# Attention of the last two layers as 26 bursts in a written TensorE order, its normalisation on GpSimd, and the value projection later

## The chip, the cores and the metric

The kernel runs on one core of a Trainium2 chip. A core has TensorE (PE, matrix products into the PSUM banks), VectorE (DVE), ScalarE (ACT), GpSimd (POOL) and SyncE (SP, which here issues the loads of the weights). Each engine runs its own queue of instructions in order; semaphores tie them together. The metric is the device time of one execution in microseconds, as a median of runs.

## The reference

Four layers on a sequence of 256 tokens of width 1024, all in fp32. The first two (a mixer of pooling and attention, a gated recurrence, each with a convolutional feed-forward part) are not touched. The change is in the mixer of the last two, `hybrid_layer`:

```python
proj = h @ w_in        # h = rms_norm(x); 6.3 thousand columns, split into the parts below
c_q, c_kv, k_r, d_q, d_k, d_v, s_q, s_k, s_v, gate_logits = jnp.split(proj, offs, axis=-1)
q = (rms_norm(c_q, g_q_lora) @ w_uq)            # MLA: 8 heads of 64 + 32, low rank
kv = (rms_norm(c_kv, g_kv_lora) @ w_ukv)        # keys and values of MLA; then norms and rope
o_mla = mla_attention(q, k, v_mla)              # softmax(q k^T) v, 8 heads
od = diff_attention(dq, dk, dv, ..., lam)       # (softmax_0 - lam softmax_1) v, 4 heads of 128
o_win = window_attention(wq, wk, wv, ..., sink) # band of 128, sinks, 8 query heads on 2 key heads
merged = gates[0] * (o_mla @ w_branch[0]) + gates[1] * (o_diff @ w_branch[1]) \
       + gates[2] * (o_win @ w_branch[2])       # gates = sigmoid(gate_logits)
x = x + merged @ w_out
```

After it come a feed-forward part and a gated addition, which are not touched.

## The kernel before

**Weights.** All weights of the kernel stand in one array in the order in which they are used (`_stream`), cut into chunks of at most 128 x 2048 elements. `_push` loads a chunk (SP's queue), and casts it into a high and a low half in fp32r: ScalarE writes `hi` (L260), VectorE the rest `lo` (L261), each in two pieces. `chunk` hands out the next one and keeps two ahead; `st`, `hi` and `lo` have three buffers each. A product (`mm3`, L277 to L279) is three fp32r matmuls: high by high, high by low, low by high.

**Order.** The program gives no order between independent instructions. A planner, with its own estimate of costs, gives each engine, step by step, the first instruction in program order whose inputs its estimate has as ready; what comes out is the fixed queue of that engine. `InOrder` is a wrapper that pins an instruction behind the one traced before it on its engine. Before, TensorE is pinned nowhere in the mixer but for the matmuls within one `chained`, so the planner strews the gates' products among the attention.

**The mixer, `hybrid`.** In program order: norm, the low-rank projection (`mla_prep`), diff queries and keys (`proj` with `headnorm`), transposes of the low-rank vector (`mla_low_rank`, L954 to L957: ScalarE writes the high half, VectorE the low half), the diff values `dv`, the MLA heads (`mla_heads`), the window keys and values (`window_kv`, keys with `headnorm`), the window queries `wq`, and then the attention: MLA in 4 pairs of heads, differential attention in 2 pairs, the windows in 4 pairs. For each pair: transposes of queries and keys (`qk_T`, L860), scores (`scores` L878, `scores2` through `chained` L870), a softmax (VectorE finds the maximum, L905 or, with a bias, L909; ScalarE the exponentials and their sums, L913; VectorE the reciprocal, L917), a normalisation on ScalarE (L922), transposes of the probabilities (`transpose4`, L849) that ScalarE copies out of PSUM (L851), and the products with the values (`pv2`, L870 and L1080). Biases are made on GpSimd (L895). After that follow the gates (12 products of 8 x 2 x 3 matmuls) and the three branches, in the order of `MERGE`: gate 0, gate 1, branch 0, gate 2, branch 1, branch 2.

`headnorm` (L426 to L431) is: squares on ScalarE, a sum on VectorE, a reciprocal root of eleven tiny instructions (L330, L317, L322 to L324 three times), and a multiplication.

**Buffers.** PSUM has 8 banks: A 3 (weight products), S 2 (scores), T 2 (transposes), O 1 (outputs). Of the SBUF tiles that matter here, `s` (probabilities) has 4 buffers, `qk` 2, `pT` 2, `bias` 2, `o` 4, `hg` 8.

Of the kernel before, what the change touches and what calls it, by code (L numbers as in the profile page):

```python
# [19 lines left out]
P = 128  # L20
S = 256
# [43 lines left out]
def _stream(a):  # L65
# [11 lines left out]
    for i in range(2):  # L77
# [131 lines left out]
class Net:  # L209
    def __init__(self, ctx, tc, ap, out, shapes, vat, rat, upto=99):  # L210
# [6 lines left out]
        self.ph = "s"  # L217
        self.vec_o, self.act_o = InOrder(tc, self.nc.vector), InOrder(tc, self.nc.scalar)
# [56 lines left out]
    def mm3(self, out, ah, al, bh, bl, start, stop):  # L275
        mm = self.nc.tensor.matmul
# [62 lines left out]
    def first_norm(self):  # L339
# [6 lines left out]
        for n in range(2):  # L346
            for t in range(2):
                pt = self.bank("ST"[t])
                for e in range(4):
                    k = 4 * n + e  # L350
                    nc.tensor.transpose(pt[:, e * P:e * P + P], self.x[:, t, k * P:k * P + P], self.ident)
# [14 lines left out]
    def norm(self, gi, banks=None, update=None):  # L366
# [7 lines left out]
        for n in range(2):  # L374
            for t in range(2):
                update(t, n, banks)
            for kp in range(2):
                pt = self.bank("ST"[kp])
                for e in range(2):
                    k = 4 * n + 2 * kp + e  # L380
                    for t in range(2):
                        nc.tensor.transpose(pt[:, e * S + t * P:e * S + t * P + P], self.x[:, t, k * P:k * P + P], self.ident)
# [19 lines left out]
    def norm_rows(self):  # L402
# [4 lines left out]
        for t in range(2):  # L407
            nc.scalar.activation(dg[:, t, :], self.ident, AF.Copy, scale=self.r[:, t:t + 1])
            nc.tensor.matmul(pb[:, t * P:t * P + P], self.ones, dg[:, t, :], start=True, stop=True)
# [58 lines left out]
    def pool_attn(self):  # L468
# [20 lines left out]
        for dst, z, tag, scale in ((qT, qk[0], "S", gqk), (kT, qk[1], "T", None)):  # L489
            for t in range(2):  # L490
                pt = self.bank(tag)
                for c in range(4):
                    nc.tensor.transpose(pt[:, c * P:c * P + P], z[:, t, c * P:c * P + P], self.ident)
# [8 lines left out]
        for c in range(4):  # L502
# [16 lines left out]
            for s in probs:  # L519
                pt = self.bank("T")  # L520
                for j in range(3):
                    nc.tensor.transpose(pt[:, j * P:j * P + P], s[:, j * P:j * P + P], self.ident)
# [21 lines left out]
        for gi in range(4):  # L544
            pb = self.bank("S")
            gc = slice(gi * P, gi * P + P)
            nc.tensor.matmul(pb[:, 0:S], u[:, 0, gc], mt[:, gi, 0:S], start=True, stop=False)
            nc.tensor.matmul(pb[:, P:S], u[:, 1, gc], mt[:, gi, S:384], start=False, stop=True)
# [3 lines left out]
            nc.tensor.matmul(pb2[:, 0:S], pw[:, gi, :], pooled, start=True, stop=True)  # L552
# [133 lines left out]
    def rglru(self, gi):  # L686
# [20 lines left out]
        for jp in range(5):  # L707
# [3 lines left out]
            for e in range(2):  # L711
# [3 lines left out]
                nc.tensor.matmul(pb[:, :S], wa[:, j, :], xc, start=True, stop=True)  # L715
                nc.tensor.matmul(pb[:, S:], wx[:, j, :], xc, start=True, stop=True)
# [126 lines left out]
    def transpose4(self, p):  # L843
# [3 lines left out]
        for kb in range(2):  # L847
            for t in range(2):
                nc.tensor.transpose(pt[:, kb * S + t * P:kb * S + t * P + P], p[:, t * S + kb * P:t * S + kb * P + P], self.ident)  # L849
# [4 lines left out]
    def qk_T(self, q, k, d, gain):  # L854
# [3 lines left out]
        for j, src in enumerate((q, k)):  # L858
            for t in range(2):
                nc.tensor.transpose(pt[:d, j * S + t * P:j * S + t * P + P], src[t], self.ident)  # L860
# [5 lines left out]
    def chained(self, mms):  # L866

        last = None
        for out, lhsT, rhs, start, stop in mms:
            ins = self.nc.tensor.matmul(out, lhsT, rhs, start=start, stop=stop)  # L870
# [4 lines left out]
    def scores(self, qT, kT):  # L875
        sp = self.bank("S")
        for t in range(2):
            self.nc.tensor.matmul(sp[:, t * S:t * S + S], qT[:, t * P:t * P + P], kT, start=True, stop=True)  # L878
# [68 lines left out]
    def mla_low_rank(self, i, c):  # L947
# [3 lines left out]
        for k in range(3):  # L951
            pt = self.bank("ST"[k % 2])
            for t in range(2):
                nc.tensor.transpose(pt[:, t * P:t * P + P], c[:, t, k * P:k * P + P], self.ident)  # L954
# [61 lines left out]
    def mla(self, q4, k4, v):  # L1016
        nc = self.nc
        v_ = nc.vector
        oh, ol = self.t([P, 4, S], "o", F32R), self.t([P, 4, S], "o", F32R)
        for cc in range(4):  # L1020
            ob = self.bank("O")
            probs = []
            for h in (2 * cc, 2 * cc + 1):
                qk = self.qk_T([q4[:, t, h, :] for t in range(2)], [k4[:, t, h, :] for t in range(2)], 96, self.gm)
                probs.append(self.softmax(self.scores(qk[:96, :S], qk[:96, S:]), FULL))
            self.pv2(ob, probs, [v[:, :, h * 64:h * 64 + 64] for h in (2 * cc, 2 * cc + 1)])
            self.split(oh[:, cc, :], ol[:, cc, :], ob[:, :S])
        return oh, ol

    def pv2(self, ob, probs, vs):  # L1030

# [236 lines left out]
```

## Time and profile before

| | |
|---|---|
| median of 3 runs | 1526.07 us (1525.44 to 1526.26) |
| the profiled execution, its own time | 1526.14 us |
| its span, first to last instruction | 1524.0 us |
| TensorE busy | 1505.0 us, 99% of the span |
| VectorE busy | 1136.7 us, 75% |
| ScalarE busy | 940.6 us, 62% |
| GpSimd busy | 53.4 us, 4% |
| granted clock of TensorE | full over the span but for its last microsecond |

Busy times are sums of the instructions' durations; a matmul's end is modelled, and the next one starts before it. The distance between two starts therefore tells more of TensorE's pace than its busy time does. In the rows below PE is TensorE's matmul, PEld its weight load, and what stands after an arrow (`<-ACT s L922`) is the instruction that ended a wait.

### The profile page before, as it was taken

What the parts mean: (1) busy time and instruction counts of PE and PEld (TensorE: products, weight loads), DVE (VectorE), ACT (ScalarE), POOL (GpSimd) and SP (SyncE); (2) the same over time, 40 slices, a digit from 0 to 9 for tenths busy, and PEclk for the clock granted to TensorE, in tenths of its full rate; (3) what the DMA queues carried; (4) which work ended last, traced back from release to release, by engine and by line L of the source; (5) the groups of instructions that cost most, each with busy time, mean ns of one, the idle gap of its engine ahead of it and who ended that gap; (6) DMA issues with size and microseconds to landing.
All of it is one profiled execution on the core that took longest, in us unless ns stands there. A gap on an engine that the chain in (4) does not pass through costs nothing.

```text
span 1524.0 us, 25331 instructions
## 1 busy us (share of the span) xinstructions
PE 1505.0 (99%) x10020; PEld 1354.2 (89%) x10020; DVE 1136.7 (75%) x2197; ACT 940.6 (62%) x1683; POOL 53.4 (4%) x45
## 2 busy tenths in 40 slices
PE   8999999999999999999999999999999999999998
PEld 6789999898999998888898999988888888999986
DVE  6559777789897777876767776668886767866666
ACT  6756555685775556677665655456777674654554
POOL 0200000000000000001110000000000110000000
PEclk9999999999999999999999999999999999999999
DMA  8445555445465554432444555444542335454551
GB/s 300 161 169 189 194 194 173 160 139 193 140 221 173 192 178 173 168 138 86 156 144 172 187 190 193 174 170 173 172 166 96 143 115 194 166 194 172 189 193 55
DMA packets 37878, 257.33 MB, mean 169 GB/s; under 512 B 4384, under 2 KB 4768, under 8 KB 8320
## 3 DMA queue, kind: packets, MB, share of 16 engines
q1 hardware_dynamic: 36576, 252.38, 46.9%
q0 software_dynamic: 896, 3.28, 0.7%
q8 instruction: 78, 1.28, 0.3%
q14 instruction: 40, 0.33, 0.1%
q10 hardware_dynamic: 288, 0.07, 0.0%
HBM read 254.66 MB, written 1.05 MB: 168 GB/s over the span
## 4 chain that ended last, share of the span: by engine, by line
PE 86%; DVE 7%; ACT 4%; issue 2%; DMA 0%; SPq 0%; ACTq 0%
PE A L278 13%; PE A L277 13%; PE A L279 13%; PE S L279 6%; PE S L278 6%; PE S L277 6%; PE T L279 6%; PE T L278 6%; PE T L277 5%; DVE lo L261 2%; PE O L277 2%; PE O L278 2%; PE O L279 2%; ACT hi L260 1%; PE T L849 1%
## 5 line engine op out<-in xcount | busy, mean ns | idle before, releaser
L261 DVE TENSOR_TENSOR lo<-st,hi 128x1024 fp32r<-128x1024 f32 (+2 forms) x480 | 571.5, 1206 | 154.3 <-ACT hi L260 151.5
L260 ACT ACTIVATE hi<-st 128x1024 fp32r<-128x1024 f32 (+2 forms) x480 | 489.2, 1043 | 239.1 <-PE T L278 110.3
L279 PE MATMUL S<-xh,lo 128*128 128x256 f32 x752 | 214.0, 285 | 0.0
L278 PE MATMUL S<-xl,hi 128*128 128x256 f32 x752 | 213.1, 283 | 0.0
L277 PE MATMUL S<-xh,hi 128*128 128x256 f32 x752 | 211.8, 282 | 0.0
L279 PE MATMUL T<-xh,lo 128*128 128x256 f32 x704 | 200.3, 285 | 0.0
L278 PE MATMUL T<-xl,hi 128*128 128x256 f32 x704 | 199.8, 284 | 0.0
L277 PE MATMUL T<-xh,hi 128*128 128x256 f32 x704 | 198.9, 283 | 0.0
L278 PE MATMUL A<-xl,hi 128*128 128x256 f32 x496 | 143.6, 290 | 1.2 <-DVE xl L388 1.1
L277 PE MATMUL A<-xh,hi 128*128 128x256 f32 x496 | 144.4, 292 | 0.0
L277 PEld LDWEIGHTS S<-xh,hi 128*128 128x128 f32 x752 | 142.6, 190 | 0.1
L279 PE MATMUL A<-xh,lo 128*128 128x256 f32 x496 | 142.3, 287 | 0.0
L279 PEld LDWEIGHTS S<-xh,lo 128*128 128x128 f32 x752 | 142.1, 189 | 0.1
L278 PEld LDWEIGHTS S<-xl,hi 128*128 128x128 f32 x752 | 141.6, 188 | 0.0
L277 PEld LDWEIGHTS T<-xh,hi 128*128 128x128 f32 x704 | 133.4, 190 | 1.6
L278 PEld LDWEIGHTS T<-xl,hi 128*128 128x128 f32 x704 | 132.5, 188 | 1.5
L279 PEld LDWEIGHTS T<-xh,lo 128*128 128x128 f32 x704 | 133.0, 189 | 0.1
L277 PE MATMUL A<-hi,xh 128*128 128x512 f32 (+2 forms) x336 | 129.0, 386 | 0.2 <-ACT xh L387 0.2
L278 PE MATMUL A<-lo,xh 128*128 128x512 f32 (+2 forms) x336 | 128.5, 382 | 0.0
L279 PE MATMUL A<-hi,xl 128*128 128x512 f32 (+2 forms) x336 | 128.0, 383 | 0.0
L278 PE MATMUL A<-lo,hg 128*128 128x512 f32 x294 | 116.3, 396 | 0.5 <-DVE lo L261 0.5
L277 PE MATMUL A<-hi,hg 128*128 128x512 f32 x294 | 116.2, 395 | 0.0
(353 smaller groups left out, 2965.6 us busy)
## 6 DMA issues: line engine op xcount, KB each, us to landing
st<-in_w_dram SPq DMA_DIRECT2D x230, 1024.0 KB, 4.8
st<-in_w_dram SPq DMA_DIRECT2D x4, 832.0 KB, 4.5
st<-in_w_dram SPq DMA_DIRECT2D x2, 768.0 KB, 4.9
x<-in_x_dram SPq DMA_DIRECT2D x2, 512.0 KB, 4.9
st<-in_w_dram SPq DMA_DIRECT2D x4, 256.0 KB, 6.3
st<-in_w_dram SPq DMA_DIRECT2D x2, 512.0 KB, 3.5
w<-in_gain_dram POOLq DMA_DIRECT2D x2, 512.0 KB, 3.9
out_dram<-x SPq DMA_DIRECT2D x4, 256.0 KB, 2.0
```

Source lines behind the costliest of these rows:

```text
L260: nc.scalar.activation(hi[:, c0:c1], st[:, c0:c1], AF.Copy)
L261: nc.vector.tensor_tensor(out=lo[:, c0:c1], in0=st[:, c0:c1], in1=hi[:, c0:c1].bitcast(F32), op=ALU.subtract)
L277: mm(out, ah, bh, start=start, stop=False)
L278: mm(out, ah, bl, start=False, stop=False)
L279: mm(out, al, bh, start=False, stop=stop)
L849: nc.tensor.transpose(pt[:, kb * S + t * P:kb * S + t * P + P], p[:, t * S + kb * P:t * S + kb * P + P], self.ident)
```

## The change

- **A written order.** `self.pe` stands for TensorE. In the attention of the last two layers it is an `InOrder` wrapper, so that TensorE's queue there is the order of the program text. The attention is cut into 26 bursts of small steps (`mq`, `ms`, `mt`, `mo` of MLA: transposes of queries and keys, scores with softmax, transposes of the probabilities, values; `dqk`, `ds`, `dt`, `do`, `dn` of the differential part; `wkt`, `wqt`, `ws`, `wt`, `wo` of the windows). After each burst come one or two of 36 parts of weight products: 4 of the window queries' projection (12 matmuls of 512 columns each), 24 of the gates, 4 of branch 0 and 4 of branch 1 (24 matmuls of 256 columns each). Branch 2 follows, unpinned.
- **Normalisation.** For MLA and the windows it is done by GpSimd (`normal`), 32 instructions of 128 x 256 a layer, in place of ScalarE's L922.
- **Projections.** The diff values `dv` come after `mla_heads`, their two chunks behind the two of the MLA heads. The window queries are projected in the first four parts and no longer ahead of the attention.
- The mathematics are the same; `nc.tensor` becomes `self.pe` in all helpers, which outside of the attention is TensorE itself.

The diff, cut to its core (the lines that only replace `nc.tensor` by `self.pe` are left out):

```diff
-        for c in (o[3], o[4], o[5]):
+        for c in (o[3], o[4]):
             out += [_kt(w, 0, 4, c, c + 512), _kt(w, 4, 8, c, c + 512)]
         out.append(_kt(a["w_uq_2"][i], 0, 2, 0, 768))
         out.append(a["w_ukv_2"][i].reshape(P, 8, 2, 64).transpose(0, 2, 1, 3).reshape(P, 1, D))
+        out += [_kt(w, 0, 4, o[5], o[5] + 512), _kt(w, 4, 8, o[5], o[5] + 512)]
         out.append(_kt(w, 0, 8, o[7], o[9]))
...
+        self.pe = self.nc.tensor
...
-    def pv2(self, ob, probs, vs):
-
-        pTs = []
-        for s, r in probs:
-            self.normalise(s, FULL, r)
-            pTs.append(self.transpose4(s))
-        mms = []
-        for kb in range(2):
-            for e in (1, 0):
-                mms.append((ob[e * 64:e * 64 + 64, :S], vs[e][:, kb, :], pTs[e][:, kb * S:kb * S + S], kb == 0, kb == 1))
-        self.chained(mms)
...
+        def normal(s, r):
+            for t in range(2):
+                c = slice(t * S, t * S + S)
+                nc.gpsimd.tensor_scalar(s[:, c], s[:, c], r[:, t:t + 1], None, op0=ALU.mult)
+            return s
+        def turn(u, probs):
+            pT[u] = [self.transpose4(s) for s in probs]
...
+        def mq(c):
+            qk["m", c] = [self.qk_T([q4[:, t, h, :] for t in range(2)], [k4[:, t, h, :] for t in range(2)], 96, self.gm)
+                          for h in (2 * c, 2 * c + 1)]
+        def ms(c):
+            sps = [self.scores(z[:96, :S], z[:96, S:]) for z in qk["m", c]]
+            pr["m", c] = [normal(*self.softmax(sp, FULL)) for sp in sps]
+        def mt(c):
+            turn(("m", c), pr["m", c])
+        def mo(c):
+            values(("m", c), outs[0], c, [mv[:, :, h * 64:h * 64 + 64] for h in (2 * c, 2 * c + 1)])
...
+        def do(hp):
+            for e in range(2):
+                h = 2 * hp + e
+                od = self.bank("O")
+                for t in range(2):
+                    for kb in range(2):
+                        self.pe.matmul(od[:, t * P:t * P + P], pT["d", hp][e][:, kb * S + t * P:kb * S + t * P + P],
+                                       dv[:, kb, h * P:h * P + P], start=kb == 0, stop=kb == 1)
+                nc.scalar.activation(o[:, :, h * P:h * P + P], od[:, :S].rearrange("p (t d) -> p t d", t=2), AF.Copy)
+            if hp == 1:
+                self.headnorm(o, 4, P)
...
+        def wkt():
+            kT.append(self.window_kT(wk))
...
+        bursts = [
+            (1, f(wkt), f(mq, 0)), (1, f(ms, 0), f(mq, 1)),
+            (1, f(mt, 0), f(ms, 1)), (2, f(mq, 2), f(mo, 0)),
+            (1, f(mt, 1), f(ms, 2)), (2, f(mq, 3), f(mo, 1)),
+            (1, f(mt, 2), f(ms, 3)), (2, f(dqk, 0, 0), f(dqk, 0, 1), f(mo, 2)),
+            (1, f(mt, 3), f(ds, 0, 0)), (2, f(mo, 3)),
+            (2, f(ds, 0, 1), f(dqk, 1, 0), f(dqk, 1, 1)),
+            (2, f(ds, 1, 0)), (1, f(wqt, 0)),
+            (1, f(dt, 0), f(ds, 1, 1)), (1, f(wqt, 1), f(do, 0)),
+            (2, f(ws, 0)),
+            (1, f(dt, 1), f(ws, 1)), (2, f(wqt, 2), f(do, 1)),
+            (1, f(wt, 0), f(ws, 2)), (2, f(wqt, 3), f(wo, 0)),
+            (1, f(wt, 1), f(ws, 3)), (2, f(dn), f(wo, 1)),
+            (1, f(wt, 2)), (1, f(wo, 2)),
+            (1, f(wt, 3)), (1, f(wo, 3)),
+        ]
+        return bursts, outs
...
+        q4, k4, v = self.mla_heads(ch, cl, kr, skr)
         dv = self.proj(xh, xl, 0)
-        q4, k4, v = self.mla_heads(ch, cl, kr, skr)
         wk, wv = self.window_kv(xh, xl)
-        wq = self.proj(xh, xl, 8)
...
+        def query():
+            b = [self.bank("A"), self.bank("A")]
+            for k0 in (0, 4):
+                wh, wl = self.chunk(4, 512)
+                for t in range(2):
+                    for k in range(4):
+                        kk, c = k0 + k, slice(t * P, t * P + P)
+                        self.mm3(b[t], xh[:, kk, c], xl[:, kk, c], wh[:, k, :], wl[:, k, :], kk == 0, kk == KD - 1)
+                    yield
+            self.copy_out(b, 512, wq)
+            self.headnorm(wq, 8, 64)
+        def gate(b):
+            for jp in range(4):
+                bk = self.bank("A")
+                wh, wl = self.chunk(KD, 256)
+                for e in range(2):
+                    for k in range(KD):
+                        c = slice(e * P, e * P + P)
+                        self.mm3(bk[:, e * S:e * S + S], wh[:, k, c], wl[:, k, c], xh[:, k, :], xl[:, k, :], k == 0, k == KD - 1)
+                    if e == 0:
+                        yield
+                g = self.times_r(self.t([P, 2, S], "hg"), bk).rearrange("p e s -> p (e s)")
+                nc.scalar.activation(g, g, AF.Tanh, scale=0.5)
+                gates[b].append(g)
+                yield
+        def branch(b):
...
+        def parts():
+            yield from query()
+            for kind, b in MERGE[:-1]:
+                yield from (gate if kind == "gate" else branch)(b)
+        self.pe = InOrder(self.tc, nc.tensor)
+        part = parts()
+        for n, *burst in bursts:
+            for f, *args in burst:
+                f(*args)
+            for _ in range(n):
+                next(part, None)
+        for _ in part:
+            pass
+        self.pe = nc.tensor
+        for _ in branch(2):
+            pass
+        mh, ml = self.halves
```

## Rows read from the trace of the kernel before

**Rows 1.** The page, busy times of the engines (us, share of the span, instructions)

```profile
PE 1505.0 (99%) x10020; PEld 1354.2 (89%) x10020; DVE 1136.7 (75%) x2197; ACT 940.6 (62%) x1683; POOL 53.4 (4%) x45
```

**Rows 2.** The windows view: busy us (x instructions) per engine, clock, DMA

```profile
783.00:805.00 22.00, 22.00 (x189) 22.00 (x188) 19.25 (x24) 9.57 (x11) 0.00 (x0) 1.00 0.49 179
648.78:782.72 133.94, 130.86 (x1011) 116.38 (x1010) 93.23 (x243) 99.15 (x232) 20.05 (x14) 1.00 0.35 122
```

**Rows 3.** TensorE's timeline, a wait: start, duration, engine, line, [idle before]

```profile
729.92 0.28 PE L278 MATMUL A<-xl,hi 128*128 128x256 f32 x1
731.14 0.33 PE L849 MATMUL T<-ident,s 128*128 128x128 f32 x1 [0.95 <-ACT s L922]
```

**Rows 4.** Line L849 in the first attention stretch: its idle time until

```profile
  ACT s L922: 5.6, 9
```

**Rows 5.** The timeline from the window keys to the attention

```profile
637.57 0.40 PE L277 MATMUL A<-hi,xh 128*128 128x512 f32 x1
...
648.78 0.60 PE L860 MATMUL T<-ident,w 128*96 128x128 f32 x4
...
651.47 0.64 PE L860 MATMUL T<-ident,w 128*96 128x128 f32 x4 [0.31 <-DVE w L1011]
...
657.92 0.48 DVE L431 TENSOR_TENSOR wk<-wk,ty 128x128 f32<-128x128 f32 x2
```

**Rows 6.** Groups by line and shape on GpSimd

```profile
L895 POOL TENSOR_SCALAR bias<-distw 128x512 f32<-128x512 f32 x16 | 24.6, 1535 | 77.9 <-DVE at L909 76.0 <-DVE ty L317 1.3
...
L514 POOL TENSOR_SCALAR qk<-bias 128x384 f32<-128x384 f32 x8 | 9.7, 1225 | 49.4 <-DVE at L909 32.4 <-DMA bias<-in_causal_dram 16.9
```

**Rows 7.** The timeline from the low-rank transposes to the MLA heads

```profile
613.55 0.38 PE L954 MATMUL S<-ident,w 128*128 128x128 f32 x2
...
615.52 0.48 DVE L957 SCALAR_TENSOR_TENSOR o<-T,vec,o 128x256 fp32r<-128x256 f32 x1
...
624.92 0.34 PE L277 MATMUL A<-hi,o 128*128 128x384 f32 x1
625.09 0.33 PE L278 MATMUL A<-lo,o 128*128 128x384 f32 x1
```

**Rows 8.** Groups by line and shape on ScalarE and VectorE

```profile
L913 ACT ACTIVATE s<-S,at 128x256 f32<-128x256 f32 x32 | 14.7, 467 | 5.1 <-DVE at L905 4.9
...
L435 ACT ACTIVATE wk<-A,r 128x128 f32<-128x128 f32 x4 | 1.4, 397 | 0.0
...
L426 ACT ACTIVATE w<-wk 128x128 f32<-128x128 f32 x4 | 1.3, 320 | 0.0
...
L905 DVE TENSOR_REDUCE at<-S 128x2 f32<-128x512 f32 x16 | 11.0, 688 | 4.2 <-PE S L878 4.2
...
L427 DVE TENSOR_REDUCE ty<-w 128x2 f32<-128x128 f32 x4 | 1.1, 278 | 0.0
```

**Rows 9.** The timeline of VectorE, reciprocal root of the diff queries

```profile
606.71 0.17 DVE L330 TENSOR_SCALAR ty<-ty 128x16 f32<-128x16 f32 x1
...
609.00 0.69 DVE L431 TENSOR_TENSOR w<-w,ty 128x512 f32<-128x512 f32 x1
```

**Rows 10.** The timeline of VectorE, between steps of another reciprocal root

```profile
643.40 1.22 DVE L261 TENSOR_TENSOR lo<-st,hi 128x1024 fp32r<-128x1024 f32 x1
644.54 0.17 DVE L322 TENSOR_TENSOR ty<-ty 128x16 f32<-128x16 f32 x1
```

**Rows 11.** The timeline at the O bank, differential attention

```profile
708.67 0.60 PE L860 MATMUL T<-ident,w 128*128 128x128 f32 x4
...
708.87 0.38 ACT L1082 ACTIVATE w<-O 128x256 f32<-128x256 f32 x1 [0.57 <-PE O L1080]
```

**Rows 12.** End of the timeline, a window after it, durations of one line

```profile
1518.55 0.39 PE L279 MATMUL O<-hi,xl 128*128 128x512 f32 x1
...
1522.00:1524.00 2.00, 0.00 (x0) 0.00 (x0) 0.00 (x0) 0.00 (x0) 0.00 (x0) 0.79 0.33 124
...
L277 PE MATMUL A<-hi,xh x336: 279/392/776, 9.3 to 1516.7; 128*128 128x512 f32 x136, 128*128 128x416 f32 x16, 128*128 128x256 f32 x16
```

More of the change, by code (lines that the diff above doesn't have):

```diff
@@ L275, in mm3 @@
     def mm3(self, out, ah, al, bh, bl, start, stop):
-        mm = self.nc.tensor.matmul
+        mm = self.pe.matmul
         mm(out, ah, bh, start=start, stop=False)
@@ L551, in pool_attn @@
             pb2 = self.bank("T")
-            nc.tensor.matmul(pb2[:, 0:S], pw[:, gi, :], pooled, start=True, stop=True)
+            self.pe.matmul(pb2[:, 0:S], pw[:, gi, :], pooled, start=True, stop=True)
             sc = self.vec("pool_scale", gi)
@@ L869, in chained @@
         for out, lhsT, rhs, start, stop in mms:
-            ins = self.nc.tensor.matmul(out, lhsT, rhs, start=start, stop=stop)
+            ins = self.pe.matmul(out, lhsT, rhs, start=start, stop=stop)
             if last is not None:
@@ L1127, in window, with ws @@
+        def ws(c):
+            sps = self.scores2((qk["w", c], kT[0]))
+            pr["w", c] = []
             for g in range(2):
                 h = g * 4 + c
-                probs.append(self.softmax(sps[g], FULL, self.bias(self.distw, self.slopes(h)),
-                                          (self.row(f"sink{i}", 8)[:, h:h + 1], self.negsink[:, h:h + 1])))
-            self.pv2(ob, probs, [v[:, :, g * 64:g * 64 + 64] for g in range(2)])
-            self.split(oh[:, c, :], ol[:, c, :], ob[:, :S])
@@ L1134, in diff_window @@
-    def diff_window(self, i, z, v, q, k, wv):
-        kT = self.window_kT(k)
-        o = self.diff(z, v)
-        od = self.t([P, 4, S], "o", F32R), self.t([P, 4, S], "o", F32R)
-        ow = self.t([P, 4, S], "o", F32R), self.t([P, 4, S], "o", F32R)
-        self.window(i, q, kT, wv, *ow, range(NWF))
-        self.diff_out(o, *od)
-        self.window(i, q, kT, wv, *ow, range(NWF, 4))
-        return od, ow
+                pr["w", c].append(normal(*self.softmax(sps[g], FULL, self.bias(self.distw, self.slopes(h)),
+                                                       (self.row(f"sink{i}", 8)[:, h:h + 1], self.negsink[:, h:h + 1]))))
@@ new lines, in wt, with wo @@
+        def wt(c):
+            turn(("w", c), pr["w", c])
+        def wo(c):
+            if outs[2] is None:
+                outs[2] = out[1]
+            values(("w", c), outs[2], c, [wv[:, :, g * 64:g * 64 + 64] for g in range(2)])
+        f = lambda *z: z
+        bursts = [
[14 more added lines that the diff above has]
+        ]
@@ new lines, in hybrid @@
+        wq = self.t([P, 2, 512], "w4")
+        bursts, outs = self.heads(i, (q4, k4, v), (dq, dk, dv), (wq, wk, wv))
+        def query():
+            b = [self.bank("A"), self.bank("A")]
+            for k0 in (0, 4):
+                wh, wl = self.chunk(4, 512)
+                for t in range(2):
+                    for k in range(4):
[4 more added lines that the diff above has]
+            self.headnorm(wq, 8, 64)
@@ new lines, in gate @@
+        def gate(b):
+            for jp in range(4):
+                bk = self.bank("A")
+                wh, wl = self.chunk(KD, 256)
+                for e in range(2):
+                    for k in range(KD):
[7 more added lines that the diff above has]
+                yield
```

138 lines of the change are left out of this document (62 added, 76 removed).

## The prediction

> **What bounds the kernel now.** I read the page first. TensorE's row says busy for 99% of the span [rows 1], so a change that adds no product and takes none away can only gain where TensorE waits, and lose where it is made to wait. The two attention stretches, one a layer, are where the change works; I read the first and take the second as like it. The windows view [rows 2] gives 133.94 us for it, in which TensorE was busy 130.86: it stood idle for 3.08 us. A busy mark hides part of each wait. In the plain stretch of the same view 189 products took 22.00 us, one per 0.1164 us, while each is drawn 0.28 us long; the timeline of one wait [rows 3] shows a gap of 731.14 - 729.92 = 1.22 us between two starts, of which 1.10 us is lost, and marks 0.95. So about 0.16 us is hidden per wait. What TensorE waits for stands in the view of the transposes' line [rows 4]: ScalarE's normalisation of the probabilities (L922), 9 times in the stretch, weight loads and products counted together. 3.08 + 9 x 0.16 = 4.5 us a layer. **That is all the present order loses there, about 9 us in two layers**, 0.6% of the kernel. The rest of the stretch is work: 672 weight products (12 x 48 of the gates, 96 of the first branch) x 0.1164 = 78.2 us, and some 340 small products and transposes that no order shortens.
>
> A rule bears on this reading. The Trainium skill, "Trainium Kernel Development and Optimization", section Performance Expectations, says matmul busy time is a bad metric because matmuls are pipelined. By busy time alone the gain would end at 3.1 us a layer, by starts at 4.5; the trace agrees with the page, since the same gap is 0.95 by one and 1.10 by the other.
>
> **What the change removes.** With 36 parts of weight products between the bursts (4 of the query projection, 12 x 0.2335 = 2.8 us each by its 48 products from 637.57 to 648.78 [rows 5]; 32 of 24 x 0.1164 = 2.8 us) nearly every softmax has far more cover than it needs. Scores of MLA pair c+1 are followed by 1 + 2 parts and two other groups before they are transposed, 10 us; the windows' by some 15 us. ScalarE also loses 32 normalisations a layer. I take the whole 4.5 us a layer as saved: **-9.0 us**. Bounds: 0 if new waits replace them, -11 if smaller gaps go too.
>
> GpSimd takes the 32 normalisations. No such shape runs there before; 512 columns take 1.54 us and 384 take 1.23 [rows 6], a straight line gives 0.9 for 256 (an estimate), so 29 us a layer on an engine that has little to do. That is free wherever the cover is 10 us. Bounds: half and the whole of the 512-column row, 0.8 to 1.5 each; neither outlasts the cover.
>
> **What it adds, a layer.**
>
> (a) The value projection moves behind the MLA heads. Before, it fills the time between the transposes of the low-rank vector (last pair at 613.55) and the heads' first product (624.92) [rows 7]. After, nothing else is ready: the casts of its chunk wait for a weight buffer that the key projection has just freed. The second low half that the first group needs starts at 615.52 and takes 0.48, so at 616.0. The six products of that group then end at about 616.3; unhindered, at the 0.17 us between 624.92 and 625.09, they would end at 613.7 + 6 x 0.17 = 614.7. **+1.6**, bounds 0.5 (other order on ScalarE and VectorE) and 2.8.
>
> (b) The first burst begins with `wkt`, the transposes of the window keys. Their projection is now the last thing before it, and TensorE's written order lets nothing pass. Before, the query projection (11.2 us) and part of MLA lay between: the keys' normalisation was done only at 657.92 + 0.48 [rows 5], 20 us after their last product, and nobody minded. What must follow the last key product: 0.2 us until ScalarE begins, a copy (0.40), the square (0.32), a reduction (0.28) [rows 8], eleven tiny instructions of the reciprocal root, as the diff queries' took 609.00 - 606.71 = 2.29 us [rows 9], and two multiplications of together 0.48 [rows 5]: 4.0 us. On ScalarE a copy of the values can slip in, on VectorE the low half of a cast, as the trace shows it doing ahead of a step of just such a chain (643.40 to 644.54), 1.22 us where a step takes 0.21 [rows 9, 10]. One of these, 1.0 us more: **+5.0**. Bounds: 4.0, and 8 with four. Queued behind `wkt` is all of TensorE. The MLA heads' own preparation is no later: before, its last step lets TensorE go at 651.47 [rows 5], 19.6 us after the heads' last product (637.57 less 48 x 0.119, 631.9); the projections of values and window keys cover 11.2 + 5.7 = 16.9 of it, with one chunk less to cast in between, two low halves of 1.22 [rows 10], so it is done within 0.3 us of their end.
>
> (c) The first scores (second burst) have only `mq(1)` and one part before `mt(0)`: 0.9 + 2.8 us, and 0.4 more until the second head's transposes. Needed: a reduction of 0.69, four exponentials of 0.47 [rows 8], a tiny reciprocal, and GpSimd's four multiplications, the last of which ends near 5.2 us after the first scores. **+1.2**, bounds 0.5 and 2.4 (a cast's low half of 1.22 us in VectorE's way).
>
> (d) There is one O bank, and `do` writes it twice in a row. Before, ScalarE's copy of the first head ends at 708.87 + 0.38 = 709.25, and four transposes use most of the 0.58 us from 708.67 until then [rows 11]; after, they stand elsewhere and the gap is bare: 0.3 to 0.58 more each, I take 0.44, twice a layer. **+0.9**, bounds 0.6 and 3.3 if a cast (1.22 at most) stands ahead of each copy.
>
> The single parts ahead of `mo`, `wo` and the last windows (2.8 us) cover ScalarE's two copies of transposed probabilities: nothing, or 1 us at most if a cast is in the way. `branch(1)` and the query projection only change place. SP's queue carries the same chunks, two of them two places later; the weight buffers still run three deep, and attention with 101 us of products between its bursts takes chunks more slowly than before: nothing.
>
> **Sum.** -4.5 + 1.6 + 5.0 + 1.2 + 0.9 = +4.2 us a layer, +8.4 in two. The profiled execution took 1526.14 us (span 1524.0, 2.1 around it), and the median of the runs is 1526.07; I forecast 1526.1 + 8.4 = **1534.5 us**, 0.55% slower.
>
> **Rivals.** *The clock falls in wait (b).* After TensorE's last product, begun at 1518.55 and 0.39 us long, the granted clock is 0.79 of full over the window 1522 to 1524 [rows 12]: the lower level is reached at 1522 + 2 x (1 - 2 x 0.21) = 1523.2, 4.2 us after the work ended. An idle time of 5.0 us is longer. Products at the lower level take twice as long: 776 ns at most against a median of 392 [rows 12]. No row shows how long it would stay down; each 2 us of it cost 1, and with 6 us taken it is 3 us a layer: 1540.5. Against it: the bound of 4.0. The rule beside it is the Trainium skill's, "TensorE: Matmul & The Clock Gate", section "HAM oscillation": gaps in TensorE's work send the clock back to half. The end of this trace agrees; no run here shows it in the middle of work.
>
> *The keys are ready in time* (the planner finds room for their projection ahead of the values'). Then (b) is gone: 1534.5 - 10 = 1524.5, no change. For it: only `wkt` itself is pinned, the products before it are not. Against: the planner took the projections in written order before.
>
> *Faster:* (b) gone and the chains of (a) and (c) covered too, 1526.1 - 9.0 + 1.8 = 1519. It decides at wait (b): below 0.8 us a layer, with the other terms as they are, the change wins. For it: the waits on L922 are real and each goes. Against: the 4.0 us are a sum of rows with nothing in between.
>
> *GpSimd becomes the bound:* 29 us of normalisation and 12 biases x 1.54 = 18 us in a stretch of 155 us; only if VectorE's accesses held it up threefold. I give it no chance of its own.
>
> **Chances.** Forecast (1529.2 to 1538) 0.43, clock or longer chain (to 1545) 0.19, ready keys (near 1525) 0.13, faster (1517 to 1523) 0.25. What a measurement can tell from no change is 0.2%, 3 us. The slower cases hold 0.62, no change 0.13, faster 0.25. The range 1519 to 1543 leaves out two tenths; for the forecast alone it is 1530 to 1541.
>
> **What would show it.** Right: in each layer one idle time of TensorE of 4 to 8 us ahead of the transposes of `wk`, ended by VectorE; one of about 1.5 us ahead of the heads' first products; no wait on ScalarE's normalisation; GpSimd busy about 29 us more a layer. Wrong: transposes of `wk` that follow the projection within a microsecond, waits that remain in the windows, or GpSimd instructions far over 0.9 us with transposes behind them.

## The result and the profile after

The changed kernel takes **1543.77 us** (median of 4 runs, 1543.30 to 1544.37) against 1526.16 beside it: ratio 1.0118, 95% interval 1.0105 to 1.013, so 17.6 us slower. The direction was forecast; the size (+8.4, 1534.5 us) was not, and the time lies 0.8 us above the range's upper end.

The page of the changed kernel, span and busy row, to be held against [rows 1]:

```profile
span 1541.5 us, 25346 instructions
PE 1501.8 (97%) x10020; PEld 1356.5 (88%) x10020; DVE 1144.5 (74%) x2197; ACT 914.6 (59%) x1619; POOL 122.2 (8%) x109
```

TensorE issues the same 10020 instructions and is even busy a little less, in a longer span: what grew is its idle time. The view of waits, TensorE from the low-rank transposes to the output projection of the first layer (what waited, what for, us in total, times, longest; all that goes through the written order stands under the helper's line, L207):

```profile
PE T L207 <- DVE wk L433: 10.1, 1, 10.1
PE O L207 <- ACT w L1141: 2.3, 2, 1.7
PE T L207 <- POOL s L1074: 0.6, 1, 0.6
PE A L279 <- ACT o L958: 0.5, 1, 0.5
```

The four waits that the forecast called (b), (d), (c) and (a) are all there, and the waits for ScalarE's normalisation [rows 4] are gone. But the largest of them is twice its size. The timeline of TensorE shows it bare:

```profile
638.51 0.28 PE L281 MATMUL A<-hi,xl 128*128 128x256 f32 x1
648.84 0.66 PE L207 MATMUL T<-ident,wk 128*128 128x128 f32 x2 [10.05 <-DVE wk L433]
```

From start to start 10.33 us (10.33 in the second layer too) lie between the last product of the window keys and the transposes of `wkt`. The windows view has what happens to the clock there, and the whole stretch in its last row (columns as in [rows 2]: PE, PEld, DVE, ACT, POOL, granted clock, DMA):

```profile
638.60:648.84 10.24, 0.19 (x3) 0.03 (x1) 9.59 (x33) 2.71 (x5) 0.00 (x0) 0.74 0.58 206
648.84:653.84 5.00, 5.00 (x17) 4.26 (x18) 1.32 (x4) 2.23 (x3) 0.00 (x0) 0.50 0.00 0
613.34:814.78 201.44, 188.02 (x1389) 170.90 (x1388) 147.04 (x333) 121.03 (x253) 55.02 (x46) 0.97 0.37 134
```

While TensorE stands still, VectorE is busy for 9.59 of 10.24 us: it is the engine that is waited for, and it does not idle. The granted clock falls during the wait and is 0.50, the lower level of 1.2 GHz, for the first 5.0 us of work behind it. What VectorE does is the answer to the rest. Its timeline, from the heads' products (they end where the next projection begins, at 621.72) to the keys:

```profile
621.21 1.29 DVE L433 TENSOR_TENSOR w<-w,ty 128x512 f32<-128x512 f32 x2
621.72 0.39 PE L279 MATMUL A<-hi,xh 128*128 128x512 f32 x1
...
623.33 1.22 DVE L263 TENSOR_TENSOR lo<-st,hi 128x1024 fp32r<-128x1024 f32 x1
624.46 0.55 DVE L980 TENSOR_REDUCE ty<-w 128x4 f32<-128x384 f32 x1
624.93 1.22 DVE L263 TENSOR_TENSOR lo<-st,hi 128x1024 fp32r<-128x1024 f32 x1
626.06 0.17 DVE L332 TENSOR_SCALAR ty<-ty 128x16 f32<-128x16 f32 x1
...
645.30 0.69 DVE L1013 TENSOR_TENSOR w<-kr,ty 128x512 f32<-128x512 f32 x1
645.91 0.28 DVE L429 TENSOR_REDUCE ty<-w 128x2 f32<-128x128 f32 x1
...
648.40 0.49 DVE L433 TENSOR_TENSOR wk<-wk,ty 128x128 f32<-128x128 f32 x2
```

Read it from the end. The window keys' root (645.91 to 648.89) takes 3.0 us, as forecast. In VectorE's queue it stands behind the last step of the MLA heads' preparation (L1013), which ends at 645.99; that is 7.2 us after the last product, where the forecast had 0.3. From the first step of the query root (626.06) to that end are 19.9 us. The same chain in the kernel before, with the first product after the heads' own:

```profile
626.79 2.36 DVE L261 TENSOR_TENSOR lo<-st,hi 128x1024 fp32r<-128x1024 f32 x2 [4.33 <-ACT hi L260]
...
631.54 0.17 DVE L330 TENSOR_SCALAR ty<-ty 128x16 f32<-128x16 f32 x1
...
631.88 0.28 PE L277 MATMUL A<-hi,xh 128*128 128x256 f32 x1
...
650.73 0.69 DVE L1011 TENSOR_TENSOR w<-kr,ty 128x512 f32<-128x512 f32 x1
```

It took as long, from 631.54 to 651.42. The windows view of the low halves alone (VectorE busy, number, clock, DMA) counts eight of them in the chain of the kernel before (first row) and eight in that of the changed kernel (second row):

```profile
631.54:651.42 19.88, 9.73 (x8) 1.00 0.60 223
626.16:645.99 19.83, 9.76 (x8) 0.94 0.66 239
```

So the chain is no longer; it starts later: 4.3 us after the heads' last product, where before it started 0.3 us ahead of it. In those 4.3 us stand two more low halves; the last reduction (624.46) and the first step of the root (626.06) each stand behind one. The squares that these reductions need are late as well. ScalarE's timeline in the changed kernel has why:

```profile
619.93 2.05 ACT L262 ACTIVATE hi<-st 128x1024 fp32r<-128x1024 f32 x2
621.82 0.57 ACT L979 ACTIVATE w<-w 128x384 f32<-128x384 f32 x1
...
623.06 0.53 ACT L979 ACTIVATE w<-w 128x384 f32<-128x384 f32 x1 [0.18 <-DVE ty L980]
```

Two casts of a weight chunk stand ahead of the last squares of the queries. With the value projection ahead of the heads, both engines had 11 us more to finish the differential keys (the multiplications at 621.21) and the casts before the heads' products came; VectorE even stood idle for 4.33 us ahead of the casts at 626.79.

### The profile page after: what moved, and what is told of

Read it like the earlier page. It is cut to its first block, busy times and chain, and to the rows that moved or that the text cites. A ratio compares the mean times of both kernels' runs of the same rounds, so it can differ in the third digit from the quotient of the medians.

```text
span 1541.5 us, 25346 instructions
## 1 busy us (share of the span) xinstructions
PE 1501.8 (97%) x10020; PEld 1356.5 (88%) x10020; DVE 1144.5 (74%) x2197; ACT 914.6 (59%) x1619; POOL 122.2 (8%) x109
## 4 chain that ended last, share of the span: by engine, by line
PE 92%; DVE 4%; ACT 2%; issue 1%; POOL 0%; DMA 0%; SPq 0%; DVEq 0%; ACTq 0%
PE A L207 13%; PE A L279 10%; PE A L280 10%; PE A L281 10%; PE S L281 6%; PE S L280 6%; PE S L279 6%; PE T L281 6%; PE T L280 6%; PE T L279 5%; PE T L207 2%; PE O L279 2%; PE O L280 2%; PE O L281 2%; PE S L207 2%; PE O L207 1%
## 5 line engine op out<-in xcount | busy, mean ns | idle before, releaser
L263 DVE TENSOR_TENSOR lo<-st,hi 128x1024 fp32r<-128x1024 f32 (+3 forms) x480 | 572.9, 1209 | 134.5 <-ACT hi L262 131.5
L262 ACT ACTIVATE hi<-st 128x1024 fp32r<-128x1024 f32 (+3 forms) x480 | 489.4, 1042 | 257.9 <-PE T L280 111.0
L1074 POOL TENSOR_SCALAR s<-s,at 128x256 f32<-128x256 f32 x64 | 69.9, 1108 | 649.1 <-DVE at L919 644.3
L279 PE MATMUL A<-hi,xh 128*128 128x512 f32 (+2 forms) x304 | 116.5, 385 | 0.2 <-ACT xh L389 0.2
L279 PE MATMUL A<-hi,hg 128*128 128x512 f32 x294 | 116.2, 395 | 0.0
L281 PE MATMUL A<-hi,hg 128*128 128x512 f32 x294 | 116.2, 395 | 0.0
L280 PE MATMUL A<-lo,xh 128*128 128x512 f32 (+2 forms) x304 | 116.0, 382 | 0.0
L281 PE MATMUL A<-hi,xl 128*128 128x512 f32 (+2 forms) x304 | 115.3, 381 | 0.0
L207 PE MATMUL A<-xh,hi 128*128 128x256 f32 x384 | 111.5, 290 | 0.0
```

The lines of the kernel that those rows point to most:

```text
L207: return lambda *a, **k: self.tc.keep_in_program_order(f(*a, **k))
L262: nc.scalar.activation(hi[:, c0:c1], st[:, c0:c1], AF.Copy)
L263: nc.vector.tensor_tensor(out=lo[:, c0:c1], in0=st[:, c0:c1], in1=hi[:, c0:c1].bitcast(F32), op=ALU.subtract)
L1074: nc.gpsimd.tensor_scalar(s[:, c], s[:, c], r[:, t:t + 1], None, op0=ALU.mult)
```

## The experiments

All times are medians beside runs of the kernel before on the same chip (1525.67 to 1526.12 us).

**1. `wkt` moved from the first burst to the thirteenth.**

```diff
-            (1, f(wkt), f(mq, 0)), (1, f(ms, 0), f(mq, 1)),
+            (1, f(mq, 0)), (1, f(ms, 0), f(mq, 1)),
...
-            (2, f(ds, 1, 0)), (1, f(wqt, 0)),
+            (2, f(ds, 1, 0)), (1, f(wkt), f(wqt, 0)),
```

> The changed kernel with the transposes of the window keys moved from the first burst to the thirteenth. Theory: the 10.3 us gap ahead of the first burst is VectorE's queue, in which the MLA keys are prepared first (their last step ends 7.3 us after the last projection product) and the window keys' root comes behind; so the gap shrinks to 7 to 8 us a layer, the clock still falls, and the time is 1537 to 1540. Rival, the prediction's own step: the MLA keys are ready within 0.3 us of the projections' end and only the window keys are late; then the gap and the slow clock go, and the time is near 1543.8 - 2 x 12.7 = 1518.

1536.49 us, ratio 1.0069 (1.0052 to 1.0086), 0.5 us below what the first theory gave. TensorE's timeline of this kernel, the transposes of the first MLA pair:

```profile
645.28 1.51 PE L207 MATMUL T<-ident,w 128*96 128x128 f32 x6 [7.04 <-DVE w L1013]
```

The wait falls from 10.3 to 7.3 us from start to start, and ends with L1013. Two things are late: the MLA keys by 7.3 us, and behind them the window keys by 3 more.

**2. The four parts of the query projection ahead of the first burst**, four later bursts followed by one part instead of two.

```diff
+        for _ in range(4):
+            next(part)
         for n, *burst in bursts:
...
-            (1, f(mt, 0), f(ms, 1)), (2, f(mq, 2), f(mo, 0)),
+            (1, f(mt, 0), f(ms, 1)), (1, f(mq, 2), f(mo, 0)),
...
```

> The changed kernel with the four query parts ahead of the first burst (11.2 us of products) and one part fewer behind bursts 4, 6, 8 and 10. Theory: the gap (10.2 us) and the 5 us at half clock (2.5 us) go in both layers: 1543.8 - 25.4 = 1518, up to 1522 if the thinner cover in MLA costs something; granted clock full. Rival: VectorE is the limit and the gap only moves, as more casts are in its queue: 1530 or more.

1527.97 us (1525.39 to 1528.95), ratio 1.0009 (1.0000 to 1.0018): 15.8 us of the loss are gone with a move of 11 us of products. In the profiled execution, which took 1525.66 us, the wait at `wkt` is 1.7 us and the clock stays up (1.000 in the mean). In six of the ten runs the mean granted clock is lower, 0.997, and these take 1527.93 to 1528.95 us; where it fell in them no trace shows. But the profiled execution too missed 1518 to 1522, because another wait grew; the view of waits of this kernel, same stretch:

```profile
PE T L207 <- POOL s L1074: 2.7, 4, 1.4
...
PE T L207 <- DVE wk L433: 1.3, 1, 1.3
```

The first transposes of probabilities now wait 2.7 us by marks (0.6 in the changed kernel). The timeline of VectorE and GpSimd in this kernel has what holds them:

```profile
659.01 1.29 DVE L433 TENSOR_TENSOR w<-w,ty 128x512 f32<-128x512 f32 x2
...
660.22 0.22 DVE L919 RECIPROCAL at<-at 128x2 f32<-128x2 f32 x2
...
660.48 4.66 POOL L1074 TENSOR_SCALAR s<-s,at 128x256 f32<-128x256 f32 x4 [252.59 <-DVE at L919]
```

The window queries, projected earlier now, are normalised on VectorE in the middle of the first softmax, whose reciprocals come behind their two multiplications; in the changed kernel the first reciprocal ran at 657.94 and GpSimd began at 658.20. These 2.1 us by marks and what is left at `wkt`, 1.6, make 3.7 us a layer; with them the expected 1518 becomes 1525.4, near the 1525.66 of the profiled execution.

**3. 96 idle transposes a layer in the long wait**, into an A bank that nothing reads.

```diff
+        junk = self.bank("A")
+        for n in range(96):
+            self.pe.transpose(junk[:, :P], self.x[:, 0, :P], self.ident)
```

> The changed kernel with 96 idle transposes (0.109 us each, 10.5 us) on TensorE between the window keys' projection and the first burst, writing to a bank that nobody reads. They fill the wait and do no other work. Theory: the wait stays, the clock stays full, and the 5 us at half pace are given back: 1543.8 - 5 = 1539. Rival: the slow clock costs nothing, since softmax chains bind there: 1544 or a little more.

1539.68 us, ratio 1.0089 (1.0074 to 1.0104), the granted clock 1.000 in the mean. The transposes fill the wait and end where it ended:

```profile
638.49 10.64 PE L207 MATMUL A<-ident,x 128*128 128x128 f32 x96
648.97 0.38 PE L207 MATMUL T<-ident,wk 128*128 128x128 f32 x2
```

`wkt` starts 0.13 us later than in the changed kernel and all is done 4.1 us earlier. So the fall of the clock costs 2.05 us a layer, apart from the wait itself.

**4. The same program without the fixed order** (the planner may place TensorE's instructions).

```diff
-        self.pe = InOrder(self.tc, nc.tensor)
+        self.pe = nc.tensor
```

> The changed kernel without the pins on TensorE, so that the planner orders the bursts and parts. Theory: the pins turn the late keys into idle time; the planner fills it with query and gate products, the clock stays full, and what remains is waits on the normalisation as before: 1522 to 1531. Rival: the wait is one of data, whatever the order: 1540 to 1545.

1523.25 us (10 runs), ratio 0.9981 (0.9972 to 0.9991): the long wait is gone, since the planner takes products of the queries and gates while the keys are late. Holding the order costs 20.5 us here.

**5. `normal` on ScalarE.**

```diff
-                nc.gpsimd.tensor_scalar(s[:, c], s[:, c], r[:, t:t + 1], None, op0=ALU.mult)
+                nc.scalar.activation(s[:, c], s[:, c], AF.Copy, scale=r[:, t:t + 1])
```

> The changed kernel with the 64 scalings of normal on ScalarE in place of GpSimd. Theory (GpSimd's 1.11 us for one scaling is felt only at the first softmax, where the first transposes wait some 0.8 to 0.9 us a layer; elsewhere the written order leaves slack): 1542 to 1545 us, the long wait ahead of wkt unchanged at about 10.3 us. Rival (GpSimd carries part of the loss in many places): 1536 to 1540 us. Second rival (64 scalings of about 0.4 us on ScalarE come in front of copies and casts for which TensorE waits): 1547 to 1552 us.

1543.6 us, ratio 1.0112 (1.0096 to 1.0127): no change, as the first theory had it. Where the normalisation runs makes no difference in this order. The gap at the first transposes stays, 0.77 us from start to start against 0.90, but it is now ended by VectorE's copy of transposed queries and keys (L865); so that gap is not GpSimd's alone. Whether the engine of the normalisation matters in the faster orders below was not run.

**6. A bank for each head in `do`.**

```diff
-                od = self.bank("O")
+                od = self.bank("OA"[e])
```

> The changed kernel with the second head's product in do going to an A bank instead of the single O bank. Theory (the waits of 1.96 and 0.90 us in do, 2.6 us a layer above pace, are the second head waiting for the copy out of the only O bank): they go, about 4.8 us less, 1538 to 1540 us. Rival (the wait is for a bank or a turned probability tile anyway and comes back at the next product): 1542 to 1544 us.

1537.92 us, ratio 1.0077 (1.0063 to 1.0091): 5.9 us less than the changed kernel, and both waits on L1141 are gone. The single O bank cost 2.9 us a layer.

**7. The kernel before, with the value projection behind the heads, and nothing else of the change.**

```diff
-        dv = self.proj(xh, xl, 0)
         q4, k4, v = self.mla_heads(ch, cl, kr, skr)
+        dv = self.proj(xh, xl, 0)
```

> The kernel before with one part of the change: the value projection (and its weights in the stream) behind the heads' preparation. Theory (it takes away only the cover of the low-rank normalisation, 0.65 us a layer seen in the changed kernel, up to 1.6 by the prediction; that the heads' keys are then ready later costs nothing here, since TensorE takes what is ready: wq, the gates' products): 1526.5 to 1529 us, and no idle time over 2 us between the heads' projections and attention. Rival (the later preparation is a loss under any order): 1534 us or more, with a wait of 5 us or more ahead of the first attention products.

1526.83 us, ratio 1.0003 (0.9994 to 1.0012): no difference. Where the planner may choose, the later preparation is free.

**8. Both moves and the bank together**, and two parts instead of one behind the second burst. The diffs of 1, 2 and 6, and:

```diff
-            (1, f(ms, 0), f(mq, 1)),
+            (2, f(ms, 0), f(mq, 1)),
...
-            (2, f(ds, 1, 0)),
+            (1, f(ds, 1, 0)),
```

> Changed kernel with four query parts ahead of the first burst, wkt moved to the thirteenth burst, two parts instead of one behind the second burst, and the second head of do in an A bank. Theory (the losses add: from 1528 with the query parts first, 1.6 us a layer of wait ahead of wkt, about 2.5 at the first transposes and 2.4 in do are taken away): 1513 to 1518 us, below both kernels. Rival (the wait at the first transposes is GpSimd's scaling of the first softmax, which one part more does not cover, and the parts taken from later bursts are missed there): 1521 to 1526 us.

1516.48 us, ratio 0.9938 (0.9925 to 0.9950): below both kernels, as the first theory had it. Beside (a), the waits at the first transposes are what is left, 2.4 us by marks in the first layer.

**9. The changed kernel with the value projection back ahead of the heads** (the edit of 7 the other way round).

> The changed kernel with the value projection back ahead of the MLA heads, the rest of the change kept. Theory (what wkt and the first MLA pair wait for is VectorE's chain behind the heads' products; the kernel before had it done 19.6 us after the heads' last product, and now only 5.7 us of products would cover it instead of 16.9): an idle time of 13 to 17 us ahead of wkt, half clock behind it, the 0.76 us gap at the low-rank vector gone, 1548 to 1556 us. So the later value projection is what the written order needs, not what hurts. Rival (the value projection's casts between the heads' products and the chain are what makes the keys late): idle time under 9 us, 1536 to 1541 us.

1549.93 us, ratio 1.0159 (1.0145 to 1.0173), as the first theory had it. TensorE's timeline of this kernel, from the first product after the heads':

```profile
631.70 0.28 PE L278 MATMUL A<-hi,xh 128*128 128x256 f32 x1
...
652.05 0.66 PE L206 MATMUL T<-ident,wk 128*128 128x128 f32 x2 [14.49 <-DVE wk L432]
```

and VectorE's, the first step of the query root and the last of the preparation:

```profile
631.36 0.17 DVE L331 TENSOR_SCALAR ty<-ty 128x16 f32<-128x16 f32 x1
...
648.52 0.68 DVE L1012 TENSOR_TENSOR w<-kr,ty 128x512 f32<-128x512 f32 x1
```

The chain starts 0.3 us ahead of the end of the heads' products (631.70) again, carries six low halves, and ends 17.5 us behind that end. That is close to the 17.2 us that the forecast worked with: they hold where the value projection stands ahead. From start to start the wait is 14.8 us. The later value projection is therefore no part of the loss: with it behind the heads the wait is 4.4 us shorter. Placed ahead of them it lets the chain begin earlier, but leaves only the window keys' products to cover it.

**10. Six low-half casts less** (three chunks of weights fetched during the values' and window keys' projections; their products take the high half twice, so the kernel leaves out what the low halves add to the result).

```diff
+        self.bare = True
         dv = self.proj(xh, xl, 0)
         wk, wv = self.window_kv(xh, xl)
+        self.bare = False
...
-            nc.vector.tensor_tensor(out=lo[:, c0:c1], in0=st[:, c0:c1], in1=hi[:, c0:c1].bitcast(F32), op=ALU.subtract)
+            if not self.bare:
+                nc.vector.tensor_tensor(out=lo[:, c0:c1], in0=st[:, c0:c1], in1=hi[:, c0:c1].bitcast(F32), op=ALU.subtract)
```

> The changed kernel without the low-half casts of the three chunks of weights that are fetched while the values and window keys are projected (six casts of 1.22 us on VectorE; the products with these low halves take the high halves instead, so that part of the result is left out and the number of products stays). Theory (VectorE is busy without a break from the heads' products to wkt, and eleven low halves stand in its queue ahead of the window keys' last step, where the forecast assumed one): the idle time ahead of wkt falls from 10.3 us by about the 7.3 us of the casts, to 3 to 5 us, the clock stays up, 1526 to 1531 us. Rival (the chain waits for ScalarE's squares and casts, or for its own small steps): the idle time stays at 8 us or more, 1538 to 1543 us.

1534.74 us, ratio 1.0059 (1.0045 to 1.0073); between the two theories. (By the timeline of the changed kernel ten low halves, not eleven, stand between the end of the heads' products and the window keys' last step.) VectorE's timeline of this kernel:

```profile
636.86 0.68 DVE L1015 TENSOR_TENSOR w<-kr,ty 128x512 f32<-128x512 f32 x1
...
640.47 1.22 DVE L265 TENSOR_TENSOR lo<-st,hi 128x1024 fp32r<-128x1024 f32 x1
...
641.68 1.22 DVE L265 TENSOR_TENSOR lo<-st,hi 128x1024 fp32r<-128x1024 f32 x1
...
643.99 0.49 DVE L435 TENSOR_TENSOR wk<-wk,ty 128x128 f32<-128x128 f32 x2
```

Without the casts in it, the heads' preparation ends at 637.54, before the last window product (638.27), as the forecast had assumed for the changed kernel. The wait that is left is 6.16 us, and two low halves stand inside the window keys' own root. That is 4.2 us less a layer, 8.3 in two, and 1543.77 less 8.3 is 1535.5. The clock still falls (0.50 for 5.54 us behind the wait); without that, 4.1 us by experiment 3, the time would lie within 1526 to 1531.

**11. Number 8 with one more part ahead of the first transposes**, taken from the burst of `ws(0)`.

```diff
-            (2, f(ms, 0), f(mq, 1)),
+            (3, f(ms, 0), f(mq, 1)),
...
-            (2, f(ws, 0)),
+            (1, f(ws, 0)),
```

> The combined order (query parts first, wkt late, second A bank in do) with one more part of products ahead of the first transposes of probabilities, taken from the burst of ws(0). Theory (3.3 and 1.4 us of gaps in front of the first transposes are a chain that is only 2 to 3 us late): these gaps fall under 1 us and no other appears, 1513 to 1515 us. Rival (the part brings its own cast and VectorE and ScalarE fall back by as much, or it is missed at the windows): 1516 to 1518 us.

**1513.03 us** (1512.54 to 1513.12), ratio **0.9915** (0.9902 to 0.9929): the fastest version, 12.6 us below the kernel before and 30.7 below the changed one, as the theory had it. Its page and its waits in the first stretch:

```profile
PE 1495.9 (99%) x10020; PEld 1353.7 (90%) x10020; DVE 1139.8 (75%) x2197; ACT 912.8 (60%) x1619; POOL 120.4 (8%) x109
```

```profile
PE O L207 <- ACT pT L853: 0.6, 1, 0.6
PE A L279 <- ACT o L958: 0.5, 1, 0.5
PE T L207 <- ACT pT L853: 0.2, 1, 0.2
```

In this stretch nothing waits for GpSimd, for VectorE or for the O bank any more; the wait of 0.6 us for ScalarE's copy of turned probabilities (L853) is new.

**12. Number 8 without the fixed order.**

> The combined order without the fixed order on TensorE: the same program, but the planner may place the products. Theory (once the inputs are ready in time, the written order is worth something: left to the planner, waits of 0.5 to 0.9 us for normalised probabilities come back, as in the changed kernel without the fixed order, 1523.25): 1520 to 1524 us. Rival (the gain lies in the order of the program and in GpSimd's normalisation, and fixing it adds nothing): 1514 to 1518 us.

1514.77 us (1514.38 to 1519.13), ratio 0.9935 (0.9921 to 0.9948), against 0.9938 with it. The rival held: once the program stands in an order whose inputs are ready, fixing that order adds nothing that these runs can tell, and leaving it to the planner loses nothing.

## Why the forecast had the direction and missed the size

**The step that failed** is in (b): "The MLA heads' own preparation is no later ... so it is done within 0.3 us of their end." It took the distance from the heads' last product to the end of the preparation (19.6 us) over from the kernel before, less two low halves. In that kernel the chain had begun before the last product was done, since the value projection stood ahead of the heads' products [rows 7: the first of these only at 624.92]. Moved 11 us forward, the products met a VectorE that still had the differential keys and two more casts to do. The distance became 24.3 us (621.72 to 645.99) in place of 17.2, so the preparation ended 7.2 us behind the projections. Two things make up the difference: the chain began 0.3 us ahead of the end of the heads' products before and 4.3 behind it now, which is 4.7 us, and it carried eight low halves both times, not two fewer, which is 2.4. Experiment 1 shows the 7.3 us by themselves; 9 shows 17.5 us for the distance where the value projection is ahead; 10 shows that without the low halves the preparation is in time, and that the wait is then 6.16 us.

**(b)'s own chain was right.** 4.0 us, and 1.0 for each low half in the way: with the two of experiment 10 that makes 6.0, measured 6.16. In the changed kernel most of these 4 us ran beside the late preparation, and 3.0 were added to its 7.2: 10.3 us from start to start, 10.2 of them lost, in place of 5.0.

**The clock's fall was a rival and came true**: 2.05 us a layer by experiment 3, where the rival said 3. It was kept out of the sum, although the 5.0 us forecast for the wait were more than the 4.2 us that it had read at the end of the trace; the case "clock or longer chain (to 1545)" had a chance of 0.19, and 1543.77 lies there: the clock fell, and the preparation was late. That products take twice as long at the lower level was read from a row that does not show it: the product of 776 ns [rows 12] is at 9.33 us, where the windows view has the granted clock at 1.00. Behind the wait of the changed kernel, at 0.50, products of 512 columns begin 0.43 us apart (652.71, 653.14); in the kernel before they begin 0.2335 apart. What the Trainium skill says ("TensorE: Matmul & The Clock Gate", section "HAM oscillation": gaps send the clock back to half) agrees with the 0.50 of the window 648.84 to 653.84; not every gap did so, as the last section shows.

**The other terms**, a layer: (a) forecast 1.6, measured 0.65, as the gap at the heads' first product is 0.76 us from start to start where pace is 0.11; (c) 1.2, measured 0.8 (0.90 between two transposes that pace sets at 0.11), of which GpSimd is not the only cause (experiment 5); (d) 0.9, measured 2.6 by the gaps and 2.9 by experiment 6. The upper bound of (d), 3.3 with a cast ahead of each copy, came near by luck, for another reason. The timeline of the changed kernel at the longer of the two gaps:

```profile
735.83 1.06 ACT L262 ACTIVATE hi<-st 128x1024 fp32r<-128x1024 f32 x1 [0.37 <-PE A L207]
735.97 1.06 PE L207 MATMUL O<-w,pT 128*128 128x128 f32 x8
...
737.39 0.63 ACT L1240 ACTIVATE hg<-hg 128x512 f32<-128x512 f32 x1 [0.51 <-DVE hg L604]
737.93 0.46 ACT L1160 ACTIVATE qk<-T,vp 128x256 f32<-128x256 f32 x1
738.29 0.37 ACT L1141 ACTIVATE w<-O 128x256 f32<-128x256 f32 x1
...
738.72 1.16 PE L207 MATMUL O<-w,pT 128*128 128x128 f32 x8 [1.69 <-ACT w L1141]
```

The cast ends at 736.89, before the first head's products do (737.03), and holds nothing up. Ahead of the copy in ScalarE's queue stand a gate's tanh (L1240), which waits for VectorE until 737.39, and a copy of transposed queries (L1160); the copy begins 1.26 us after the products' end.

**What the change removes** was put at 4.5 us a layer and was larger. The stretch grew by 201.44 - 192.34 = 9.1 us (192.34 from 613.11 to the same product at 805.45 in the kernel before). The losses above are 10.2 + 2.05 + 0.65 + 0.8 + 2.6 = 16.3, so some 7.2 were saved; this is the remainder and not a measurement of its own. Experiment 11, which of these losses has only (a) left, is 12.6 us faster than the runs beside it, 6.3 a layer, 7.0 with (a). That is beyond the bound of 11 us in two layers. The waits of [rows 4] are gone as forecast. The rest lies inside what the page counts as busy: 1505.0 us before [rows 1] and 1495.9 in experiment 11, for the same 10020 instructions. Parts of 24 or 48 products on end change less often between products and transposes than the order before; that this is the whole of it was not tested. It does not come from holding the order: in experiment 12, where the planner orders the same parts, TensorE is busy for 1495.8 us.

**GpSimd as the bound** was given no chance, rightly: experiment 5.

By term, two layers: forecast 2 x (-4.5 + 1.6 + 5.0 + 1.2 + 0.9) = +8.4; measured 2 x (-7.2 + 0.65 + 10.2 + 2.05 + 0.8 + 2.6) = +18.2, against 17.6 by the time of the runs (with the -7.2 a remainder, this holds for the stretch as a whole and says nothing of the single terms). The forecast had both sides too small, the losses at 17.4 us in place of 32.6 and the gain at 9.0 in place of 14.4, and these two errors partly cancel: with the gain as small as forecast the change would have been some 5 us slower still. The direction came from the right place, the wait ahead of `wkt`. The gain of the change is real and larger than forecast; the written order gives back 12.3 us a layer for these 7.2 in one place, where it starts with the input that is ready last.

## What to carry to other kernels

A fixed order on the busiest engine turns every late input into idle time, so list for each group when its inputs are ready in the *new* order, and follow the whole queue of the engine that makes them, casts of later weights included; a distance from the old trace does not move along with the products. Begin such an order with work whose inputs are long there: 11 us of products moved ahead gave back 15.8 us here. And compare a fixed order with the same program left to the planner, since the better order may already be worth all of it (experiments 8 and 12).

## What the runs showed of the hardware

- The half-speed time behind a wait did not follow the length of the wait. In the two layers the granted clock was 0.50 for 5.54 and 5.35 us after waits of 6.2 us (experiment 10), 3.64 and 3.27 after 7.3 (experiment 1), 5.00 and 4.21 after 10.3 (the changed kernel), 3.93 and 3.59 after 14.8 and 14.6 (experiment 9). The 1.7 us of experiment 2's profiled execution and the 1.96 us of the changed kernel's `do` left the clock at 1.00. But without one long wait the clock can fall too; experiment 4, windows:

```profile
660.00:664.65 4.65, 3.15 (x16) 1.89 (x16) 2.24 (x5) 1.71 (x8) 3.97 (x4) 1.00 0.03 12
664.65:668.06 3.41, 3.41 (x16) 2.33 (x16) 1.45 (x5) 2.76 (x9) 1.92 (x3) 0.50 0.00 0
```

TensorE was busy for 3.15 of 4.65 us, with gaps of at most 0.9 us from start to start, and then ran 3.41 us at half.

- GpSimd's scaling of 256 columns took 0.92 us each at the first softmax of the changed kernel, close to the estimate of 0.9 from [rows 6], but 1.11 in the mean of all 64. The view by tile of the first stretch of probabilities, and the group of the whole kernel:

```profile
L1074 POOL TENSOR_SCALAR s<-s,at x4: 922/924/924, 658.2 to 660.9; 128x256 f32<-128x256 f32 x4
```

```profile
L1074 POOL TENSOR_SCALAR s<-s,at 128x256 f32<-128x256 f32 x64 | 69.9, 1108 | 649.1 <-DVE at L919 644.3 <-ACT s L915 4.3
```

What slows the others was not separated.
